# Tree attention on one Trainium2 core: products and transposes in couples of 64 columns, without the side-by-side copies

## The chip, the cores and the metric

The kernel runs on one core of one Trainium2 chip. The time is device time in microseconds (us), the median of several executions. The profile is one further execution, taken with the hardware profiler. Engines are named as the profile names them: PE is TensorE (PEld its weight loads), DVE is VectorE, ACT is ScalarE, POOL is GpSimd, SP is SyncE. "L561" is line 561 of the kernel.

## The reference

Attention over 8 x 12 = 96 heads of 512 positions by 64 numbers, fp32 in and out. Position i is a node of a binary tree and sees only itself and its ancestors:

```python
scale = 1.0 / np.sqrt(dim)
mask = np.zeros((seq, seq))
for i in range(seq):
    mask[i, i] = 1
    parent = i
    while parent > 0:
        parent = (parent - 1) // 2
        mask[i, parent] = 1
scores = np.einsum('bhqd,bhkd->bhqk', Q, K) * scale
scores = scores + (1 - mask) * (-1e9)
weights = np.exp(scores - np.max(scores, axis=-1, keepdims=True))
weights = weights / (np.sum(weights, axis=-1, keepdims=True) + 1e-10)
return np.einsum('bhqk,bhkd->bhqd', weights, V).astype(np.float32)
```

## The kernel before

The 96 heads are worked in 48 pairs; a pair's two heads lie on partitions 0 to 63 and 64 to 127 wherever 64 numbers of a head are the contraction. Four pairs (8 heads) are a group, the unit of loading: `load_k` and `load_q` bring 8 heads of K or Q, `load_v` 8 heads of V, from fp32 in memory to bf16 on the chip, all issued from GpSimd's queue. Results go out in fp32, 8 heads a store (`store`), and pair by pair for the last group (`store_pair`).

A pair passes through these steps:

- **Transposes** (`transpose_rows` for K, `transpose_coarse` for Q; L384 and L406, and L359 for the first group). TensorE turns K and Q of a group into columns, in four steps for a group, two of K and two of Q. VectorE copies the result out of PSUM (`evac`, tile `kq`). From group 3 on, a copy first lays the rows of two heads side by side (`lay_beside`, tiles `Kbeside` and `Qbeside`, L333), so that one transpose has 128 columns of weights and writes all 128 partitions: 8 transposes a step. In groups 0 to 2 there is no copy, and two transposes of 64 columns each write one half of the partitions: 16 a step. The copies of Q are GpSimd's, those of K VectorE's in groups 3 to 5 and GpSimd's from 6 on.
- **Scores** (`scores1`, `scores2`; L503, L508, L528, L534). Each query needs only a few blocks of keys. Codes added by extra products push the forbidden places far down. ScalarE takes the exponentials (L519, L550) into the tiles `e1` and `e2`.
- **Values** (`values`, L561). The exponentials are the weights of the array, 65 columns of V with a one behind them stream through; the 65th column of the result is the sum. For each head four products take `e1`, all 128 columns wide. Of the four that take `e2`, those with t = 2 and 3 are 128 wide; for t = 0 and 1 the two halves of the queries need different tiles of V (`SELF`), so each is two products of 64 columns. That is 20 products a pair, the 64-wide ones of both heads last.
- **Norm** (`norm`, L594 and L599): VectorE divides by the sum.

V is laid into five slots by copies of 32 or 64 partitions (`spread`, L309), shared out among GpSimd, VectorE and ScalarE by tables.

The order on each engine is written out by hand (`manual_schedule`): the main loop runs over pairs, with the steps S (scores of pair i), T (one step of transposes, some pairs ahead) and V (values and norm of pair i - 1); X is a filling product. GpSimd's order is the list of `pool_program`, one queue of loads, spreads, copies and stores in a fixed sequence; `ready` decides at which pair an entry may be written into the program. Loaded K and Q lie in `loads`, three buffers each, so a load of group g needs the buffer of group g - 3, which is free once that group's copy side by side is done. Stores are put some eight groups behind the loads (`BEHIND`), so in the last part of the kernel stores alone move.

Of the kernel before, what the change touches and what calls it, by code (L numbers as in the profile page):

```python
# [12 lines left out]
CODE_BITS = 16  # L13
NOUT = 10
BEHIND = 64
LANES = 8
COARSE = range(1, 12)
COARSE_K = range(1, 12)
BESIDE = {"K": range(3, 12), "Q": range(3, 12)}
K_BY_POOL = range(6, 12)  # L20


UNITS = (
# [101 lines left out]
def kernel(  # L125
# [36 lines left out]
    ctx.enter_context(tc.manual_schedule())  # L162

    consts = ctx.enter_context(tc.tile_pool(name="consts", bufs=1))
    loads = ctx.enter_context(tc.tile_pool(name="loads", bufs=3))
    beside = ctx.enter_context(tc.tile_pool(name="beside", bufs=2))
    vloads = ctx.enter_context(tc.tile_pool(name="vloads", bufs=3))
    work = ctx.enter_context(tc.tile_pool(name="work", bufs=2))
    etpool = ctx.enter_context(tc.tile_pool(name="etpool", bufs=3))
# [144 lines left out]
        for part in ((), (4, 5), (4, 5), (4, 5, 2))[min(o, 3)]:  # L314
            spread(nc.gpsimd.tensor_copy, o, part, h0, h1)

    besides = {}

    def lay_beside(copy, name, g):

        kept = (ksts if name == "K" else qsts)[g]
        to = besides[name, g] = beside.tile([P, GP, 4, 2, D], bf16, name=f"{name}beside")
        dst = to[:, :, :, :, :].bitcast(mybir.dt.uint32)
        src = kept[:, :, :, :].bitcast(mybir.dt.uint32)
        if g not in COARSE:
            src = src.rearrange("p (x a) t w -> p x t a w", a=2)
        elif name == "Q" or g in COARSE_K:
            src = src.rearrange("p a s w -> p s a w")
        else:
            src = src.rearrange("p (a x) t w -> p (x t) a w", a=2)  # L330
        if g in COARSE:
            dst = dst.rearrange("p x t a w -> p (x t) a w")
        copy(out=dst, in_=src)  # L333

    def lay_q(g):
        lay_beside(nc.gpsimd.tensor_copy, "Q", g)

    def lay_early(g):
        lay_beside(nc.gpsimd.tensor_copy, "K", g)

    halves_of, every = [slice(64 * a, 64 * a + 64) for a in range(2)], slice(0, P)

    def turned(name, g, t, both, single):

        if g in BESIDE[name]:
            return [(every, both(besides[name, g]).rearrange("p a d -> p (a d)"))]
        return [(halves_of[a], single(a)) for a in range(2)]

    def transpose_one(dst, rows, units, src, perm):

# [10 lines left out]
    def transpose_keys(i, kqp, half):  # L361
        g, x = divmod(i, GP)
        assert all(("kst", head(i, a)) in issued for a in range(2))
        for t in range(4):
            for rows, src in turned(
                "K", g, t, lambda b: b[:, x, t, :, :], lambda a: ksts[g][:, head(i, a) % KB, t, :]
            ):
                transpose_one(kqp[:, half, :, :], rows, _slot_layout(t)[1], src, perms[t])

    def transpose_rows(i, x):  # L370

        g = i // GP
        for half in range(2):
            j = 2 * x + half
            for t, (units, perm) in enumerate(runs):
                for rows, src in turned(
                    "K", g, t, lambda b: b[:, j, t, :, :], lambda a: ksts[g][:, a, 4 * j + t, :]
                ):
                    dst = kqps[i][rows, half, units[0], :]
                    dst = bass.AP(  # L380
                        dst.tensor, dst.offset,
                        [list(dst.ap[0])] + [[32 * (u - units[0]), 2] for u in units[2:0:-1]] + [[1, 32]],
                    )
                    nc.tensor.transpose(out=dst, in_=src, identity=perm)  # L384

    def transpose_coarse(i):

        g, x = divmod(i, GP)
        kqps[i] = kqps[i - 1] if x == 3 else psT.tile([P, 2, 32, 32], bf16, name="kqp")
        if x < 2 and g in COARSE_K:  # L390
            assert all(("kst", h) in issued for h in range(KB * g, KB * g + KB))
            return transpose_rows(i, x)
        if x < 2:
            for half in range(2):
                transpose_keys(GP * g + 2 * x + half, kqps[i], half)
            return
        assert all(("qst", h) in issued for h in range(KB * g, KB * g + KB))
        for half in range(2):
            for y, t in enumerate(ORDER):
                four = 2 * x - 4 + half  # L400
                for rows, src in turned(
                    "Q", g, t, lambda b: b[:, four, t, :, :], lambda a: qsts[g][:, a, 4 * four + t, :]
                ):
                    u = 16 * half + y
                    dst = kqps[i][rows, x - 2, u:u + 13:4, :]
                    nc.tensor.transpose(out=dst, in_=src, identity=eye[:, 0:128])  # L406

    def transpose(i, halves=(0, 1)):
        g = i // GP
        if g in COARSE:  # L410
            return transpose_coarse(i)
        if 0 in halves:
            kqps[i] = psT.tile([P, 2, 32, 32], bf16, name="kqp")
            transpose_keys(i, kqps[i], 0)
        assert all(("qst", h) in issued for h in (2 * i, 2 * i + 1))
        for y, t in enumerate(ORDER if 1 in halves else ()):
            for rows, src in turned(
                "Q", g, t, lambda b: b[:, i % GP, t, :, :], lambda a: qsts[g][:, 2 * i % KB + a, t, :]
            ):
                units = [2 * y, 2 * y + 1, 2 * y + 9, 2 * y + 10]  # L420
                transpose_one(kqps[i][:, 1, :, :], rows, units, src, qperm)

# [129 lines left out]
    def values(i):  # L552
# [4 lines left out]
            obs[i] = ob = psS.tile([P, 2, 512], fp32, name="s1")  # L557
        e1, e2, vt = ets[i], e2s[i % NE], vts[(2 * i // VB) % NV]

        def product(e, a, t, tile_v, lo=0, hi=128, **flags):  # L560
            nc.tensor.matmul(  # L561
                out=ob[lo:hi, a, 65 * t:65 * t + 65],
                lhsT=e[:, a, PLACE[t], lo:hi],
# [1 line left out]
                **flags,  # L565
            )

        def halves(a):
            for t in (0, 1):
                product(e2, a, t, 1 + SELF[t], 0, 64, start=False, stop=t == 1)  # L570
                product(e2, a, t, 1 + t, 64, 128, start=False, stop=t == 1)

        for a in range(2):
            for t in range(4):
                product(e1, a, t, 0, start=t == 0, stop=False)
            for t in (2, 3):
                product(e2, a, t, 1 + t, start=False, stop=False)
            if i == NP - 1:
                halves(a)
        if i < NP - 1:  # L580
            for a in range(2):
                halves(a)

    def norm(i):
        g = i // GP
# [34 lines left out]

    def pool_program():

        K_BEFORE = {
            6: (load_k, 8 * KB, KB), 10: (spread_top, 5, 0, KB), 11: (store, nc.gpsimd, 5),
        }

        Q_BEFORE = {
            3: (load_k, 5 * KB, KB), 4: (load_k, 6 * KB, KB), 5: (spread_top, 3, 0, KB), 6: (spread_top, 3, KB, VB),
            9: (spread_top, 4, KB, VB), 10: (spread_top, 5, KB, VB),
        }  # L630
        ops = [
            (load_k, 2, 2), (load_q, 2, 2), (load_v, 0, 8), (load_k, 4, 4),
            (load_q, 4, 2), (load_q, 6, 2), (load_k, 8, 8), (load_q, 8, 8), (eye_order,),
# [22 lines left out]
        ops.append((spread_top, NH // VB - 1, KB, VB))  # L656
        ops += [(store, nc.gpsimd, q) for q in range(stored, NH // KB - 1)]
        ops += [(store_pair, nc.gpsimd, i) for i in (NP - 4, NP - 3)]
        for g in BESIDE["Q"]:
            if g in Q_BEFORE:  # L660
                ops.insert(ops.index(Q_BEFORE[g]), (lay_q, g))
                continue
            at = ops.index((load_q, KB * g, KB)) + 1
            behind = 0
            while behind < LANES:
                behind += {load_k: 1, load_q: 1, load_v: 1, store: 2, store_pair: 1}.get(ops[at][0], 0)
                at += 1
            ops.insert(at, (lay_q, g))
        for g in K_BY_POOL:
            before = K_BEFORE.get(g, (lay_q, g))  # L670
            ops.insert(ops.index(before), (lay_early, g))
        return ops

    def ready(op, i):

        f, args = op[0], op[1:]
        if f in (load_k, load_q):
            g = args[0] // KB - 3
            name = "K" if f is load_k else "Q"
            return (name, g) in besides if g in BESIDE[name] else done >= GP * (g + 1)  # L680
        if f in (code_order, eye_order):
            return True
        if f in (lay_q, lay_early):
            return done >= GP * (args[0] - 1)
        if f is load_v:
            return 2 * i >= args[0] + args[1] - 3 * VB
        if f is spread_top:
# [58 lines left out]
                out=tile[:, 0, :], lhsT=idle[:, 0:128], rhs=idle[:, :], start=True, stop=True  # L746
            )

    def lay_k(i):

        for g in BESIDE["K"]:
            if g not in K_BY_POOL and i == K_TURN.get(g, GP * g - 7):
                lay_beside(nc.vector.tensor_copy, "K", g)

    spin("s1", 9)
    for kept, name, src in ((ksts, "kst", "K"), (qsts, "qst", "Q")):
        kept[0] = loads.tile([P, KB, 4, D], bf16, name=name)
        nc.vector.tensor_copy(out=kept[0][:, 0:2, :, :], in_=first[src][:, :, :, :])
    TWICE = (9,)
    K_TURN = {3: 7, 4: 10, 5: 14}  # L760
    FIRST = ['XKSQ', 'SXXXKXQDVAT', 'SVATT', 'SVTT', 'STV', 'STVD']
    done = 1
    pool(-1)
# [3 lines left out]
    for i in range(NP + 1):  # L767
        steps = FIRST[i] if i < len(FIRST) else "STVT" if i in TWICE else "SVT" if i == 8 else "STV"
        for n, step in enumerate(steps):
# [7 lines left out]
            if step == "T" and done < NP:  # L777
                transpose(done)
                evac(done)
                done += 1  # L780
                if "T" not in steps[n + 1:]:
                    lay_k(i)
            if step == "K":
                transpose(done, (0,))
            if step == "Q":
# [10 lines left out]
            spread_by(nc.vector.tensor_copy, BY_VECTOR, STEADY_VECTOR, i)  # L796
        if "A" not in steps:
            spread_by(nc.scalar.copy, BY_SCALAR, STEADY_SCALAR, i)
        if "T" not in steps:
            lay_k(i)  # L800
        pool(i)
        if i == NP - 1:
            store_pair(nc.sync, NP - 2)
# [33 lines left out]
```

## Time and profile before

| what | value |
|---|---|
| time, median of 3 runs | 133.08 us (133.0 to 133.45) |
| span of the profiled execution, first to last instruction | 131.9 us |
| what the median has beyond that span | 1.2 us |
| granted TensorE clock, mean | 0.993 |
| PE busy | 115.4 us in 2130 matmuls and transposes |
| DVE, ACT, POOL busy | 99.8, 94.1, 96.0 us |
| HBM read and written | 37.86 and 12.58 MB |

The profiled execution's own time is known as its span; what lies around the span is taken as the 1.2 us in the table. A row of the profile's groups reads: line, engine, operation, result <- operands, shapes, count, then busy time, mean duration of one in ns, then the engine's idle time just before and what ended it. Matmuls overlap each other, so a row's length is from the first's begin to the last's end. A row of the timeline or the chain reads: begin, length (us), engine, line, operation. Names such as `128*64 128x65` mean contraction rows * columns of the weights, then partitions x streamed columns.

### The profile page before, as it was taken

Reading aid. Unit: us, or ns where it says so; the run is one execution under the profiler, and the core shown is the slowest. Engines: PE = TensorE matmul, PEld = TensorE weight load, DVE = VectorE, ACT = ScalarE, POOL = GpSimd, SP = SyncE. Lnnn points to the kernel's source line nnn. Section 1 sums busy time; section 2 is a strip of 40 time slices with the busy share of each in tenths; the row PEclk is TensorE's granted clock in tenths of the full one; section 3 lists DMA queues with packets and bytes.
Section 4 is the critical chain, followed back from the end, with each engine's and each line's share of the span. In section 5 each row is a group of like instructions: output and inputs, shape, how many; then the busy total and the mean of one; then the engine's idle time right before and its main releaser. Section 6 shows DMA issues by size and latency. Waiting matters only on the chain.

```text
span 131.9 us, 4944 instructions
## 1 busy us (share of the span) xinstructions
PE 115.4 (88%) x2130; PEld 82.4 (62%) x2131; DVE 99.8 (76%) x191; ACT 94.1 (71%) x154; POOL 96.0 (73%) x147
## 2 busy tenths in 40 slices
PE   4989968899799879699999998999999999989930
PEld 1443645667566657477777776786877777856620
DVE  4339957774996897987988979879888799775460
ACT  4339345797766695778977889587888897979910
POOL 6999546049589899999999999699699998202300
PEclk9999999999999999999999999999999999999997
DMA  3999999999999999999999999999999989999991
GB/s 115 201 181 194 212 195 217 195 211 204 208 200 211 205 208 201 211 202 212 205 207 207 220 342 221 208 341 228 209 325 245 299 352 391 370 381 404 375 366 66
DMA packets 24533, 32.13 MB, mean 244 GB/s; under 512 B 944, under 2 KB 15920, under 8 KB 24512
## 3 DMA queue, kind: packets, MB, share of 16 engines
q0 software_dynamic: 23232, 30.67, 110.2%
q1 hardware_dynamic: 720, 0.70, 1.6%
q10 hardware_dynamic: 560, 0.46, 1.1%
q8 instruction: 16, 0.26, 0.7%
q14 instruction: 5, 0.04, 0.1%
HBM read 37.86 MB, written 12.58 MB: 382 GB/s over the span
## 4 chain that ended last, share of the span: by engine, by line
PE 63%; DVE 25%; ACT 6%; issue 3%; ACTq 0%
PE ob L561 18%; PE s L503 8%; PE kqp L406 8%; DVE of L599 7%; DVE kq L445 6%; PE s L508 6%; PE kqp L384 6%; PE s L528 6%; PE s L534 5%; DVE vt L309 4%; PE s L745 3%; ACT e L550 3%; ACT e L519 2%; PE kqp L359 2%; DVE kq L453 2%
## 5 line engine op out<-in xcount | busy, mean ns | idle before, releaser
L519 ACT ACTIVATE e<-s 128x1024 bf16<-128x1024 f32 x48 | 49.1, 1023 | 28.1 <-PE s L508 27.9
L309 POOL COPY vt<-vst 32x256 uint32<-32x256 uint32 (+2 forms) x70 | 36.1, 516 | 10.1 <-DMA vst<-in_V_dram 6.9
L550 ACT ACTIVATE e<-s 128x384 bf16<-128x384 f32 (+1 forms) x92 | 41.4, 505 | 0.0
L561 PE MATMUL ob<-vt,e 128*128 128x65 bf16 (+1 forms) x940 | 37.3, 197 | 3.2 <-DVE of L599 2.4
L561 PEld LDWEIGHTS <-e 128*128 128x128 bf16 (+1 forms) x960 | 31.2, 102 | 9.4 <-DVE of L599 4.8
L599 DVE TENSOR_TENSOR of<-ob,rec 128x512 f32<-128x512 f32 x44 | 30.4, 691 | 1.5
L309 DVE COPY vt<-vst 32x512 uint32<-32x512 uint32 (+4 forms) x43 | 23.2, 539 | 1.2
L594 DVE RECIPROCAL rec<-ob 128x8 f32<-128x8 f32 x47 | 9.5, 203 | 14.3 <-PE ob L561 13.5
L534 PEld LDWEIGHTS <-kq 64*128 64x128 bf16 x384 | 16.1, 110 | 6.4
L508 PE MATMUL s<-kq 64*128 64x512 bf16 x96 | 18.4, 378 | 1.3 <-DVE kq L445 1.3
L534 PE MATMUL s<-kq 64*128 64x160 bf16 (+1 forms) x384 | 17.8, 210 | 0.0
L503 PE MATMUL s<-qcoarse,codes 40*128 40x512 bf16 x88 | 17.2, 387 | 0.0
L528 PE MATMUL s<-qcoarse,codes 40*128 40x480 bf16 x88 | 16.3, 364 | 0.4 <-ACT e L550 0.2
L453 DVE COPY kq<-kqp 128x1024 bf16<-128x1024 bf16 x22 | 15.1, 687 | 2.0 <-PE kqp L384 1.3
L607 POOL DMA_DIRECT2D out_dram<-of x11 | 9.8, 893 | 8.5 <-DVE of L599 8.5
L445 DVE COPY kq<-kqp 128x2048 bf16<-128x2048 bf16 x11 | 13.5, 1224 | 2.4 <-PE kqp L406 1.8
L528 PEld LDWEIGHTS <-codes 40*128 40x128 bf16 x96 | 7.5, 95 | 9.1 <-issue 2.0
L384 PE MATMUL kqp<-mixed,Kbeside 128*128 128x128 bf16 x144 | 11.1, 220 | 1.8 <-DVE Kbeside L333 1.2
L333 POOL COPY Qbeside<-qst 128x1024 uint32<-128x1024 uint32 x9 | 9.7, 1081 | 2.6 <-DMA qst<-in_Q_dram 2.5
L406 PE MATMUL kqp<-ptile,Qbeside 128*128 128x128 bf16 x144 | 11.1, 220 | 0.4 <-DVE kq L453 0.4
L260 POOL DMA_DIRECT2D vst<-in_V_dram x12 | 10.9, 907 | 0.0
L384 PEld LDWEIGHTS <-Kbeside 128*128 128x128 bf16 x144 | 8.3, 98 | 3.2 <-DVE Kbeside L333 1.5
(45 smaller groups left out, 97.7 us busy)
## 6 DMA issues: line engine op xcount, KB each, us to landing
out_dram<-of POOLq DMA_DIRECT2D x11, 1024.0 KB, 9.9
vst<-in_V_dram POOLq DMA_DIRECT2D x12, 512.0 KB, 14.4
kst<-in_K_dram POOLq DMA_DIRECT2D x11, 512.0 KB, 12.2
qst<-in_Q_dram POOLq DMA_DIRECT2D x11, 512.0 KB, 13.2
out_dram<-ol POOLq DMA_DIRECT2D x2, 256.0 KB, 5.3
qst<-in_Q_dram POOLq DMA_DIRECT2D x3, 128.0 KB, 7.6
ol<-in_K_dram SPq DMA_DIRECT2D x1, 256.0 KB, 2.9
ol<-in_Q_dram ACTq DMA_DIRECT2D x1, 256.0 KB, 3.6
```

What stands on the lines that cost most here:

```text
L309: return copy(out=dst, in_=src)
L384: nc.tensor.transpose(out=dst, in_=src, identity=perm)
L406: nc.tensor.transpose(out=dst, in_=src, identity=eye[:, 0:128])
L445: return nc.vector.tensor_copy(out=dst, in_=src) if x == 3 else None
L503: nc.tensor.matmul(out=columns(g, sp[:, a, :], 0, 512), lhsT=k1code[64 * a:64 * a + CODE_ROWS, :], rhs=query_codes(i, a, 0, 0, 512), start ...
L508: nc.tensor.matmul(out=columns(g, sp[:, a, :], 0, 512), lhsT=keys(i, a, TOP), rhs=queries(i, a, 0, 512), start=False, stop=True,)
L519: nc.scalar.activation(out=dst, in_=src, func=AF.Exp, scale=scale)
L528: nc.tensor.matmul(out=columns(g, flat[:, a, :], 32, 512), lhsT=k2code[64 * a:64 * a + CODE_ROWS, :], rhs=query_codes(i, a, 1, 32, 512), s ...
L534: nc.tensor.matmul(out=columns(g, flat[:, a, :], lo, hi), lhsT=keys(i, a, TILE2[t]), rhs=queries(i, a, lo, hi), start=False, stop=t == 1,)
L550: nc.scalar.activation(out=dst, in_=src, func=AF.Exp, scale=scale)
L561: nc.tensor.matmul(out=ob[lo:hi, a, 65 * t:65 * t + 65], lhsT=e[:, a, PLACE[t], lo:hi], rhs=vt[:, head(i, a) % VB, tile_v, 0:D + 1], **flags,)
L599: nc.vector.tensor_tensor(out=dst, in0=o4[:, a:a + n, :, 0:D], in1=rec[:, a:a + n, :, :].to_broadcast([P, n, 4, D]), op=ALU.mult,)
```

## The change

Every transpose of K and Q and every value product becomes two of 64 columns, one for each half of the partitions. A pair takes 32 value products in place of 20, and a step of transposes 16 in all groups. The copies side by side, their buffers and their places in GpSimd's and VectorE's order go; the transposes of groups 3 to 11 read the loaded tiles themselves. `loads` has five buffers in place of three, and a load may be written once the transposes of five groups before have been. In the value step, all products of one head stand before those of the other, the `e1` products first.

```diff
-LANES = 8
-BESIDE = {"K": range(3, 12), "Q": range(3, 12)}
-K_BY_POOL = range(6, 12)
+LOADED = 5
...
-    loads = ctx.enter_context(tc.tile_pool(name="loads", bufs=3))
-    beside = ctx.enter_context(tc.tile_pool(name="beside", bufs=2))
+    loads = ctx.enter_context(tc.tile_pool(name="loads", bufs=LOADED))
...
-                for rows, src in turned(
-                    "K", g, t, lambda b: b[:, j, t, :, :], lambda a: ksts[g][:, a, 4 * j + t, :]
-                ):
+                for a, rows in enumerate(halves_of):
+                    src = ksts[g][:, a, 4 * j + t, :]
...
-                for rows, src in turned(
-                    "Q", g, t, lambda b: b[:, four, t, :, :], lambda a: qsts[g][:, a, 4 * four + t, :]
-                ):
+                for a, rows in enumerate(halves_of):
+                    src = qsts[g][:, a, 4 * four + t, :]
...
-        def halves(a):
-            for t in (0, 1):
-                product(e2, a, t, 1 + SELF[t], 0, 64, start=False, stop=t == 1)
-                product(e2, a, t, 1 + t, 64, 128, start=False, stop=t == 1)
-
         for a in range(2):
             for t in range(4):
-                product(e1, a, t, 0, start=t == 0, stop=False)
-            for t in (2, 3):
-                product(e2, a, t, 1 + t, start=False, stop=False)
-            if i == NP - 1:
-                halves(a)
-        if i < NP - 1:
-            for a in range(2):
-                halves(a)
+                for lo in (0, 64):
+                    product(e1, a, t, 0, lo, lo + 64, start=t == 0, stop=False)
+            for t in range(4):
+                for lo, of in ((0, SELF[t]), (64, t)):
+                    product(e2, a, t, 1 + of, lo, lo + 64, start=False, stop=t == 3)
...
-        for g in BESIDE["Q"]:
...
-            ops.insert(at, (lay_q, g))
-        for g in K_BY_POOL:
-            before = K_BEFORE.get(g, (lay_q, g))
-            ops.insert(ops.index(before), (lay_early, g))
         return ops
...
         if f in (load_k, load_q):
-            g = args[0] // KB - 3
-            name = "K" if f is load_k else "Q"
-            return (name, g) in besides if g in BESIDE[name] else done >= GP * (g + 1)
+            return done >= GP * (args[0] // KB - LOADED + 1)
```

More of the change, by code (lines that the diff above doesn't have):

```diff
@@ L315, in spread_top @@
             spread(nc.gpsimd.tensor_copy, o, part, h0, h1)
[L317 to L347, printed above, removed]
+    halves_of = [slice(64 * a, 64 * a + 64) for a in range(2)]
     def transpose_one(dst, rows, units, src, perm):
@@ L364, in transpose_keys @@
         for t in range(4):
-            for rows, src in turned(
-                "K", g, t, lambda b: b[:, x, t, :, :], lambda a: ksts[g][:, head(i, a) % KB, t, :]
-            ):
+            for a, rows in enumerate(halves_of):
+                src = ksts[g][:, head(i, a) % KB, t, :]
                 transpose_one(kqp[:, half, :, :], rows, _slot_layout(t)[1], src, perms[t])
@@ L400, in transpose_coarse @@
                 four = 2 * x - 4 + half
-                for rows, src in turned(
-                    "Q", g, t, lambda b: b[:, four, t, :, :], lambda a: qsts[g][:, a, 4 * four + t, :]
-                ):
+                for a, rows in enumerate(halves_of):
+                    src = qsts[g][:, a, 4 * four + t, :]
                     u = 16 * half + y
@@ L416, in transpose @@
         for y, t in enumerate(ORDER if 1 in halves else ()):
-            for rows, src in turned(
-                "Q", g, t, lambda b: b[:, i % GP, t, :, :], lambda a: qsts[g][:, 2 * i % KB + a, t, :]
-            ):
+            for a, rows in enumerate(halves_of):
+                src = qsts[g][:, 2 * i % KB + a, t, :]
                 units = [2 * y, 2 * y + 1, 2 * y + 9, 2 * y + 10]
@@ L558, in values, with product @@
         e1, e2, vt = ets[i], e2s[i % NE], vts[(2 * i // VB) % NV]
-        def product(e, a, t, tile_v, lo=0, hi=128, **flags):
+        def product(e, a, t, tile_v, lo, hi, **flags):
             nc.tensor.matmul(
@@ L621, in pool_program @@
     def pool_program():
[L623 to L630, printed above, removed]
         ops = [
@@ L658, in pool_program @@
         ops += [(store_pair, nc.gpsimd, i) for i in (NP - 4, NP - 3)]
-        for g in BESIDE["Q"]:
[L660 to L667, printed above, removed]
-            ops.insert(at, (lay_q, g))
-        for g in K_BY_POOL:
-            before = K_BEFORE.get(g, (lay_q, g))
-            ops.insert(ops.index(before), (lay_early, g))
         return ops
@@ L677, in ready @@
         if f in (load_k, load_q):
-            g = args[0] // KB - 3
-            name = "K" if f is load_k else "Q"
-            return (name, g) in besides if g in BESIDE[name] else done >= GP * (g + 1)
+            return done >= GP * (args[0] // KB - LOADED + 1)
         if f in (code_order, eye_order):
             return True
-        if f in (lay_q, lay_early):
-            return done >= GP * (args[0] - 1)
         if f is load_v:
@@ L747, in spin @@
             )
[L749 to L753, printed above, removed]
     spin("s1", 9)
@@ L759 @@
     TWICE = (9,)
-    K_TURN = {3: 7, 4: 10, 5: 14}
     FIRST = ['XKSQ', 'SXXXKXQDVAT', 'SVATT', 'SVTT', 'STV', 'STVD']
@@ L780 @@
                 done += 1
-                if "T" not in steps[n + 1:]:
-                    lay_k(i)
             if step == "K":
@@ L798 @@
             spread_by(nc.scalar.copy, BY_SCALAR, STEADY_SCALAR, i)
-        if "T" not in steps:
-            lay_k(i)
         pool(i)
```

## The prediction

> **What bounds the kernel now.** I read the page first: the engines' shares, the slices and the chain that ended last.
>
> ```profile
> span 131.9 us, 4944 instructions
> ...
> PE 115.4 (88%) x2130; PEld 82.4 (62%) x2131; DVE 99.8 (76%) x191; ACT 94.1 (71%) x154; POOL 96.0 (73%) x147
> ...
> DMA  3999999999999999999999999999999989999991
> GB/s 115 201 181 194 212 195 217 195 211 204 208 200 211 205 208 201 211 202 212 205 207 207 220 342 221 208 341 228 209 325 245 299 352 391 370 381 404 375 366 66
> ...
> q8 instruction: 16, 0.26, 0.7%
> ...
> PE 63%; DVE 25%; ACT 6%; issue 3%; ACTq 0%
> ```
>
> Two things are full at once. TensorE is busy 88% of the span and carries 63% of the chain. The DMA line reads 9 in nearly every slice from the second to the last but one. The rate in the first half, about 205 GB/s, is bf16 as written, so the fp32 read behind it is about 410 GB/s; in the eight slices before the last one fp32 results move, at 352 to 404 GB/s. So the DMA engines have no pause to give back, wherever it is that TensorE gets faster. The view by windows, for the last two stretches, shows where this ends:
>
> ```profile
> core 0: us, PE busy (x) PEld busy (x) DVE busy (x) ACT busy (x) POOL busy (x), PEclk, DMA share, GB/s
> 112.00:126.00 14.00, 13.08 (x263) 9.35 (x260) 8.78 (x19) 12.40 (x21) 3.20 (x4) 1.00 1.01 385
> 126.00:131.90 5.90, 0.39 (x10) 0.22 (x7) 1.46 (x5) 0.00 (x0) 0.00 (x0) 0.85 0.51 189
> ```
>
> From 112 to 126 us the stores run at 385 GB/s; in the last 5.90 us 189 GB/s, or 5.90 x 189 = 1.12 MB, are still moved. At 385 GB/s those would take 2.9 us, so with all results ready in time the bulk would be out at 126.0 + 2.9 = 128.9. The end of the present chain is this (timeline, and the view of DMA issues from 120 us on):
>
> ```profile
> 127.65 0.35 ACTq L616 DMA_DIRECT2D out_dram<-ol  x1
> ...
> out_dram<-of POOLq DMA_DIRECT2D x1, 1024.0 KB, 7.1
> ...
> out_dram<-ol ACTq DMA_DIRECT2D x1, 128.0 KB, 3.0
> ```
>
> The last store of a whole group lands 7.1 us after its issue, behind earlier ones. The very last store is issued at 127.65 and lands in 3.0 us, at 130.65; the span ends 1.25 us after that. It found no queue. So the end is set by the compute chain, but the DMA's own end is right under it: 128.9 for the bulk against 130.65 for the last landing.
>
> **The value products.** A pair now takes 12 products of 128 columns and 8 of 64; it will take 16 couples of 64. The timeline of one pair, cut by narrow windows so that the row shows only what had begun, an early pair that is followed by a half-width transpose, and one product by itself:
>
> ```profile
> 73.04 0.54 PE L561 MATMUL ob<-vt,e 128*128 128x65 bf16 x12
> 73.51 0.28 PE L561 MATMUL ob<-vt,e 128*64 128x65 bf16 x6
> 73.51 0.32 PE L561 MATMUL ob<-vt,e 128*64 128x65 bf16 x8
> ...
> 16.37 0.79 PE L561 MATMUL ob<-vt,e 128*128 128x65 bf16 x20
> 16.99 0.22 PE L384 MATMUL kqp<-mixed,kst 128*64 128x128 bf16 x2
> ...
> 75.17 0.19 PE L561 MATMUL ob<-vt,e 128*128 128x65 bf16 x1
> ```
>
> Twelve full products end at 73.58; with 0.19 us for one, the last begins at 73.39, so they follow at 0.35/11 = 0.032 us. The first half product begins at 73.51, 0.12 us after it and not 0.03: a change of width costs about 0.09 us. The fourth couple lengthens its row from 0.28 to 0.32; the whole row holds three steps, (0.32 - 0.19)/3 = 0.043 on average, the first of them the longest, since couples 2 to 4 can load weights behind running ones only once one runs. I take the later step as 0.032, that of a full product, which streams the same 65 columns, with 0.030 and 0.043 as ends. Sixteen couples then take 0.32 + 12 x 0.032 = 0.70 us against 0.79: a saving of 0.09 (0.11 at 0.030; at 0.043 the row is 0.84, a loss of 0.05).
>
> On weight loads the Trainium skill speaks against the change: the page "TensorEngine Tiling (Array Packing)", section Restrictions, says that column tiling rules out the fast weight load, and "TensorE: Matmul & The Clock Gate" gives a load as columns/1.2 ns, by which I estimate 53 ns for 64 columns and, if that were each couple's step, a pair of about 1.0 us. The rows above show steps far below that once couples run.
>
> **The transposes.** Groups 1 and 2 have the half form already, later groups the full one, so the profile shows both:
>
> ```profile
> 24.17 0.64 PE L384 MATMUL kqp<-mixed,kst 128*64 128x128 bf16 x16
> 24.74 0.20 PE L561 MATMUL ob<-vt,e 128*128 128x65 bf16 x1
> ...
> 74.71 0.62 PE L384 MATMUL kqp<-mixed,Kbeside 128*128 128x128 bf16 x8
> ```
>
> Sixteen halves take 0.64 us, eight fulls 0.62: +0.02 for a pair. With 0.22 for one transpose (the row at 16.99), the last half begins at 24.59 and the full product 0.15 later; the last full one begins at 75.11 and the product, at 75.17, 0.06 later. So the half form before full products costs 0.09 in a change of width. After the change products are half too and this falls away: in the 16.37 row products end at 17.16, the last begins at 16.97, and the half-width transpose begins 0.02 later. I charge nothing for it, so the step stays at 0.06 as now for groups 3 to 11. The scores stay as they are, and a change of width on entering and leaving them stays.
>
> The sum for a pair in the steady stretch is -0.09 + 0.02 = -0.07 us on TensorE (ends -0.09 and +0.07). What a pair takes now is in the chain:
>
> ```profile
> 86.70 0.61 PE ob L561 x20
> ...
> 88.82 0.61 PE ob L561 x20
> ...
> 125.36 1.04 PE s L561 x20
> ```
>
> A pair lasts 88.82 - 86.70 = 2.12 us, and all pieces between are TensorE's. From about 55 to 117 us the chain goes on like this, with some 28 such pairs: 28 x 0.07 = 2.0 us. The last pair changes width three times within 1.04 us; as 16 couples it takes 0.70, another 0.3 us on the very end.
>
> **Copies and buffers.** These rows (groups by form, and the waits) price what goes:
>
> ```profile
> L384 PE MATMUL kqp<-mixed,Kbeside 128*128 128x128 bf16 x144 | 11.1, 220 | 1.8 <-DVE Kbeside L333 1.2 <-DVE kq L445 0.3 <-DVE kq L453 0.3
> L406 PE MATMUL kqp<-ptile,Qbeside 128*128 128x128 bf16 x144 | 11.1, 220 | 0.4 <-DVE kq L453 0.4
> L333 POOL COPY Qbeside<-qst 128x1024 uint32<-128x1024 uint32 x9 | 9.7, 1081 | 2.6 <-DMA qst<-in_Q_dram 2.5
> L333 DVE COPY Kbeside<-kst 128x1024 uint32<-128x1024 uint32 x3 | 2.1, 687 | 0.0
> PEld L384 <- DVE Kbeside L333: 1.5, 2, 1.0
> ```
>
> VectorE loses three copies, 2.1 us, all before 55 us, and TensorE the 1.5 us it waits for two of them there. Part of that wait stands beside VectorE work that stays, so I count 1.0 (0 to 1.5). GpSimd loses nine Q copies, 9.7 us, and six K copies of like size. GpSimd is on no chain; what it gains is that loads and stores behind a copy are issued sooner. Their order in its one queue does not change: the copies are taken out of the list and all else stays. With a DMA queue that is never empty, a sooner issue lands nothing sooner. With three buffers a load waits for a copy of three groups before, with five for the transposes of five groups before, which were done long ago. So the buffers are worth 0 by themselves; they are what the longer-kept inputs need. If the queue ran dry somewhere, it would be around 105 us, and that would be a gain of a few tenths at most.
>
> TensorE's instructions rise: 576 more products (48 pairs x 12) and 288 more transposes, each with its weight load, 4261 to about 5990. The page has 16 fetches of instructions at 0.7% of 16 engines' span: 0.007 x 16 x 131.9 / 16 = 0.9 us of one DMA engine each. Seven more are 6.5 us of one engine, 0.4 us spread over sixteen; this delays the floor by 0.4 (0 if they fit into gaps, 0.9 if one falls on the engine that ends last).
>
> **The sum.** By the chain: -2.0 - 1.0 - 0.3 = -3.3 us. By the DMA: the bulk can be out at 128.9 + 0.4 = 129.3; if the last small stores land some 0.6 us behind it, at 129.9 where they now land at 130.65, and the 1.25 us after the landing stay, the span is 131.2. So of 3.3 us about 0.7 come through (0 to 1.7, the ends being no use of the floor's slack, and a last landing at 128.9 with no fetch charged). The median shown, 133.08, is 1.2 over the profiled span; I carry the difference over and round to 132.4.
>
> **Rivals.** (a) Nothing comes through: the fetches and the tail of small stores eat the 0.7. For it: DMA at 9 throughout, and the last 5.90 us already hold stores that queue for 7.1 us. Against: the last one lands in 3.0. It gives 132.7 to 133.4, so 133.0. (b) Slower: TensorE is not supplied with instructions or weights at the rate that sixteen couples want. A pair's products become 64 instructions, four for each couple; that is 0.032/4 = 0.008 us each, while the longest runs in the trace need one in 0.016 (twelve full products with their loads) or 0.42/32 = 0.013 (the sixteen half transposes). The four couples seen follow a pause of 0.12 us in which instructions can collect. It decides where a couple's step passes 0.039 us (0.79 - 0.02 - 0.19 = 0.58 over 15 steps). At 0.043 throughout, a pair loses 0.07, over 28 to 47 pairs 2 to 3.3 us: 135 to 136.4. At 0.013 per instruction a couple takes 0.052, the pair loses 0.20, and the time is 138.7 to 142.5. Against it: the fourth couple's step is 0.04 rounded, and the scores before each run leave time to collect. (c) The DMA is no floor: GpSimd's copies slowed it, and all 3.3 us come through: 129.8. The windows speak against it: from 112 to 126 us GpSimd works 3.20 of 14 us, and the DMA moves 385 GB/s, no more than the 410 before.
>
> The skill's rule that fits the gain is in "TensorEngine Tiling (Array Packing)", Key Properties: a change of tiling mode drains TensorE. The 0.12 against 0.03 above agrees.
>
> **How the numbers follow.** The forecast (the DMA lets through 0.7) has 0.52, (a) 0.21, (b) 0.21, (c) 0.06. A measurement of this kernel tells some 0.3% (0.4 us) from no change, so faster is below 132.7. The forecast's own range is 131.7 to 133.0, a tenth to a fifth of it above 132.7: faster 0.43 + 0.06 = 0.49; same 0.09 + 0.18 = 0.27; slower 0.03 + 0.21 = 0.24. The range runs from 131.6 to 136.4: it leaves out (c) and the harder half of (b), under 2 in 10.
>
> **What would show it.** Right: a product row of about 0.70 for 32 instructions and no pause of 0.12 within; half transposes of 0.64 followed by products after 0.06; pairs of 2.05 us; TensorE done some 3 us before its 126.4 of now, and the last store queueing for longer than 3.0 us. Wrong: couples that step by more than 0.039, idle time of TensorE put down to issue, a wait of transposes for K loads (then the loads have become late), or a DMA that shows gaps and an end that moves by 2 us or more.

## The result, and the profile after

The changed kernel takes 151.14 us (149.92 to 152.69, four runs) against 133.26 for the kernel before: a ratio of 1.129, 95% interval 1.119 to 1.139. It is slower by 18 us, where 0.7 us of gain were forecast. Each ratio here and below leaves out runs that are over 1.5% above the fastest of their kernel and goes by runs of the kernel before taken beside them, so it need not be the ratio of two medians shown. The profiled execution spans 148.5 us in place of 131.9. Its page:

```profile
span 148.5 us, 6661 instructions
...
PE 114.3 (77%) x2994; PEld 82.5 (56%) x2995; DVE 95.5 (64%) x188; ACT 94.3 (64%) x154; POOL 78.9 (53%) x132
...
DMA  4999999999999999999999999999708998043284
...
q8 instruction: 23, 0.38, 1.0%
...
PE 58%; issue 13%; DMA 10%; DVE 8%; ACT 5%; POOL 3%; ACTq 0%; POOLq 0%
```

TensorE is not busier than before (114.3 against 115.4 us), though it has 2994 matmuls and transposes in place of 2130. It stands still more. "issue", time in which the engine waited for nothing that the profile shows, was 3% of the chain and is 13%, and DMA, which was not in the chain, is 10%. The fetches of instructions rose from 16 to 23, as forecast. The waits say where TensorE stood:

```profile
PE ob L524 <- issue: 11.3, 8, 2.3
...
PE s L497 <- issue: 3.7, 2, 2.2
...
PE kqp L349 <- issue: 2.6, 2, 1.5
...
PE kqp L349 <- DMA kst<-in_K_dram: 1.7, 1, 1.7
...
PE kqp L370 <- issue: 1.5, 1, 1.5
PE s L471 <- issue: 1.0, 1, 1.0
```

Fifteen gaps of 0.5 to 2.3 us, 21.8 us in all, in value products, scores and transposes alike. They bear no relation to what the program does at that place. The timeline shows one, in the middle of a row of products, and a row without one:

```profile
56.84 0.67 PE L524 MATMUL ob<-vt,e 128*64 128x65 bf16 x32
...
58.95 0.60 PE L524 MATMUL ob<-vt,e 128*64 128x65 bf16 x27
61.10 0.26 PE L524 MATMUL ob<-vt,e 128*64 128x65 bf16 x5 [1.54 <-issue]
...
62.23 0.64 PE L370 MATMUL kqp<-ptile,qst 128*64 128x128 bf16 x16
62.71 0.68 PE L524 MATMUL ob<-vt,e 128*64 128x65 bf16 x32
```

An undisturbed row of 32 products takes 0.67 to 0.68 us. The row of 58.95 stops after 27 of them until 61.10. What these gaps have in common is their distance, counted in instructions. Cutting the windows at points inside the gaps (54.9, 60.8 and, at the gap before a single product at 66.92, 66.6) gives the number between them:

```profile
54.90:60.80 5.90, 4.39 (x128) 3.35 (x128) 4.16 (x8) 4.21 (x7) 5.51 (x11) 1.00 1.26 205
60.80:66.60 5.80, 4.39 (x128) 3.36 (x127) 3.57 (x6) 4.20 (x7) 4.38 (x9) 1.00 1.18 207
```

A row of such a window reads: stretch, length, then busy time and number of instructions of PE, PEld, DVE, ACT and POOL, the granted clock, the DMA's share and GB/s. 128 matmuls and 128 weight loads are 256 instructions, and a fetch of instructions is 16 KB (0.38 MB in 23), 64 bytes for each of 256. The transfer of one begins at 58.8, ends at 59.7, and TensorE goes on at 61.10; the next begins at 64.7 (DMA windows of 0.1 us there hold one packet of the instruction queue each), and TensorE goes on at 66.92. So the transfer of a block begins 3.6 us after TensorE steps into the block before it (55.17 and 61.10), takes 0.95, and 1.3 us more pass until its instructions run: 5.9 us from one block to the next, in which TensorE works for 4.39. The granted clock is 1.00 in both windows, so it is not the clock that makes them long. Where it does fall, to 0.72 from 91.5 to 97.5 us, the block takes 6.0 us as well, but TensorE is busy for 5.61 of them and no gap stands at its end.

The DMA's 10% of the chain is the same thing under another name:

```profile
76.86 14.84 DMA kst<-in_K_dram
91.69 0.20 issue
91.89 0.24 PE kqp L349
```

TensorE does stand before this transpose, but its K (group 8, issued at 58.8, 14.0 us to landing) had been there since 72.8; the load issued at 76.86 is K of group 10, which this transpose does not read. A fetch had begun at 89.5, and by count the transpose is the first instruction of a new block. In the kernel with loads cut in two, further below, the same transpose stands for the same 1.74 us, and there the profile names VectorE. So both names are the profile's guess at a wait for a block.

### The profile page after: what moved, and what is told of

The parts are those of the page before. It is cut to its first block, busy times and chain, and to the rows that moved or that the text cites. A ratio compares the mean times of both kernels' runs of the same rounds, so it can differ in the third digit from the quotient of the medians.

```text
span 148.5 us, 6661 instructions
## 1 busy us (share of the span) xinstructions
PE 114.3 (77%) x2994; PEld 82.5 (56%) x2995; DVE 95.5 (64%) x188; ACT 94.3 (64%) x154; POOL 78.9 (53%) x132
## 4 chain that ended last, share of the span: by engine, by line
PE 58%; issue 13%; DMA 10%; DVE 8%; ACT 5%; POOL 3%; ACTq 0%; POOLq 0%
PE ob L524 14%; DMA kst<-in_K_dram 10%; PE s L466 8%; PE kqp L349 7%; PE kqp L370 6%; PE s L491 6%; PE s L471 6%; PE s L497 5%; PE s L675 3%; DVE kq L408 2%; POOL vt L306 2%; ACT e L482 2%; ACT e L513 2%; PE kqp L326 2%; PE ob L675 1%
## 5 line engine op out<-in xcount | busy, mean ns | idle before, releaser
L482 ACT ACTIVATE e<-s 128x1024 bf16<-128x1024 f32 x48 | 49.2, 1024 | 43.1 <-PE s L471 42.9
L306 POOL COPY vt<-vst 32x256 uint32<-32x256 uint32 (+2 forms) x70 | 34.4, 491 | 33.9 <-PE ob L524 16.7
L524 PE MATMUL ob<-vt,e 128*64 128x65 bf16 x1504 | 34.4, 196 | 12.4 <-issue 11.3
L524 PEld LDWEIGHTS <-e 128*64 128x64 bf16 x1536 | 30.8, 112 | 14.7 <-issue 12.1
L497 PEld LDWEIGHTS <-kq 64*128 64x128 bf16 x384 | 16.9, 111 | 11.1 <-issue 4.6
L497 PE MATMUL s<-kq 64*128 64x160 bf16 (+1 forms) x384 | 18.6, 212 | 3.7 <-issue 3.7
L306 DVE COPY vt<-vst 32x512 uint32<-32x512 uint32 (+4 forms) x43 | 20.5, 477 | 1.2
L349 PE MATMUL kqp<-mixed,kst 128*64 128x128 bf16 x352 | 14.7, 225 | 5.6 <-issue 2.6
L466 PE MATMUL s<-qcoarse,codes 40*128 40x512 bf16 x88 | 17.4, 391 | 0.2 <-ACT e L482 0.2
L370 PE MATMUL kqp<-ptile,qst 128*64 128x128 bf16 x352 | 14.2, 222 | 1.8 <-issue 1.5
L349 PEld LDWEIGHTS <-kst 128*64 128x64 bf16 x352 | 11.0, 111 | 7.5 <-issue 4.4
L370 PEld LDWEIGHTS <-qst 128*64 128x64 bf16 x352 | 10.7, 109 | 3.7 <-issue 2.2
```

Source lines behind the costliest of these rows:

```text
L306: return copy(out=dst, in_=src)
L466: nc.tensor.matmul(out=columns(g, sp[:, a, :], 0, 512), lhsT=k1code[64 * a:64 * a + CODE_ROWS, :], rhs=query_codes(i, a, 0, 0, 512), start ...
L482: nc.scalar.activation(out=dst, in_=src, func=AF.Exp, scale=scale)
L497: nc.tensor.matmul(out=columns(g, flat[:, a, :], lo, hi), lhsT=keys(i, a, TILE2[t]), rhs=queries(i, a, lo, hi), start=False, stop=t == 1,)
L524: nc.tensor.matmul(out=ob[lo:hi, a, 65 * t:65 * t + 65], lhsT=e[:, a, PLACE[t], lo:hi], rhs=vt[:, head(i, a) % VB, tile_v, 0:D + 1], **flags,)
```

## The experiments

The fetch theory: where the DMA is loaded, TensorE gets 256 instructions in about 6.0 us and no more, so a group of four pairs takes at least 11.6 us after (496 instructions) and 7.9 before (336), where the group measured below took 9.0. A pair has 14 score products, 20 value products and 8 transposes before, 32 and 16 of the last two after, each with a weight load: 84 and 124 instructions. The expectations below count four too few for every pair (80 and 120, and so on), which moves their least times by 0.4 us a group and no verdict. The rivals: couples cannot be supplied for long whatever the DMA does (couple theory); or the missing copies and five buffers changed the order of loads so that something starves (buffer theory).

**One half of the change at a time.** First the value products alone as couples; then transposes, copies and buffers alone. The first (v_only) is the kernel before with this edit in `values`; the second (t_only) is the kernel after with this edit taken back:

```diff
-                product(e1, a, t, 0, start=t == 0, stop=False)
-            for t in (2, 3):
-                product(e2, a, t, 1 + t, start=False, stop=False)
-            if i == NP - 1:
-                halves(a)
-        if i < NP - 1:
-            for a in range(2):
-                halves(a)
+                for lo in (0, 64):
+                    product(e1, a, t, 0, lo, lo + 64, start=t == 0, stop=False)
+            for t in range(4):
+                for lo, of in ((0, SELF[t]), (64, t)):
+                    product(e2, a, t, 1 + of, lo, lo + 64, start=False, stop=t == 3)
```

> Only the value products become couples; transposes, side-by-side copies and three buffers stay as before. A group of four pairs then has 4 x 104 = 416 TensorE instructions (before 4 x 80 = 320, after 4 x 120 = 480). Fetch theory (TensorE streams its instructions in blocks of 256, and with the DMA busy one block takes about 6.0 us from request to use): a group cannot be shorter than 416 x 6.0 / 256 = 9.75 us, against 9.0 us in before; over 8 groups +6 us, so 137 to 142 us, with idle time of TensorE at every 256th instruction of about 0.5 to 1 us each. Buffer theory (the new order of loads and the missing copies starve the transposes): no change from before or a little faster, 132 to 133.5 us. Couple theory (a couple cannot be supplied at 0.03 us for long): the row of 32 products is itself longer than 0.79 us.

> Only the transposes become couples, the copies go and there are five buffers; value products stay 12 full and 8 half. A group has 4 x 96 = 384 instructions. Fetch theory: at least 384 x 6.0 / 256 = 9.0 us a group, just what a group takes now, plus 0.09 us per pair for the change of width between transposes and full products: 0 to +5 us, 133 to 138 us, with small stalls at every 256th instruction. Buffer theory: all of the loss is here, 148 to 152 us.

Couples of values alone: 140.22 us, ratio 1.057 (1.049 to 1.065). Transposes, copies and buffers alone: 133.51, ratio 1.003 (0.999 to 1.007), no difference that can be told. Removing the copies and adding buffers costs nothing, so the buffer theory falls; but five small gaps, 2.3 us in all, are put down to issue in its trace, where the kernel before has none in its main loop. With couples for the values alone, a value row without a gap takes 0.70 us (0.67 to 0.68 in the kernel after, 0.79 for 20 products), so couples are not slow in themselves; the gaps are there, shorter, and a block apart:

```profile
61.59 0.70 PE L561 MATMUL ob<-vt,e 128*64 128x65 bf16 x32
...
83.89 0.60 PE L561 MATMUL ob<-vt,e 128*64 128x65 bf16 x26
85.55 0.28 PE L561 MATMUL ob<-vt,e 128*64 128x65 bf16 x6 [1.05 <-issue]
...
79.20:85.20 6.00, 4.85 (x128) 3.65 (x128) 4.04 (x7) 4.00 (x8) 4.85 (x6) 1.00 1.19 211
85.20:91.30 6.10, 5.50 (x128) 4.08 (x128) 4.80 (x10) 4.14 (x7) 5.10 (x9) 1.00 1.16 295
```

**The kernel after with fewer products.** All of after, with couples on the second exponentials left out, eight (`E2_TILES` = 0) or four (2) of the sixteen, down to 92 and to 108 instructions a pair:

```diff
-            for t in range(4):
+            for t in range(E2_TILES):
                 for lo, of in ((0, SELF[t]), (64, t)):
...
```

> The kernel after, with the eight couples of each pair that take the second exponentials left out (the result is not the reference's); couples, half-width transposes, five buffers, no copies, all loads and stores stay. A pair has 88 TensorE instructions, a group 352. Fetch theory: 352 x 6.0 / 256 = 8.25 us a group would do, less than a group takes anyway, so no idle time at the 256th instructions and 131.5 to 133.5 us, that is, the loss of 18 us is gone. If the loss lies in half width, missing copies or buffers, most of it stays: 145 us or more.

> The same with only four of the sixteen couples of a pair left out: 104 instructions a pair, as many as the kernel with couples for the values alone. Fetch theory: 416 x 6.0 / 256 = 9.75 us a group and the time of that kernel, 138 to 142 us, although its transposes, copies and buffers are others. Any theory by kind of instruction: closer to after, 146 to 150.

With 92 instructions: 133.39 us, ratio 1.001 (0.996 to 1.005). With 108: 139.43, ratio 1.045 (1.038 to 1.052), near the couples of values alone with their 108. Two kernels with different transposes, copies and buffers agree within 1% at the same count. By kind of instruction nothing fits: eight couples a pair, and all half-width transposes, cost nothing here.

The kernels side by side. The group is measured from the first K transposes of group 3 to those of group 11, divided by 8; its instructions are twice the weight loads that the trace has between these marks, divided by 8 (the stretch holds about 31 pairs, not 32):

| kernel | instructions a pair | instructions in the measured group | group, us | us per 256 | ratio of times |
|---|---|---|---|---|---|
| before | 84 | 323 | 9.0 | 7.1 | 1 |
| after, 8 couples left out | 92 | 358 | 8.95 | 6.4 | 1.001 |
| transposes alone | 100 | 388 | 9.06 | 6.0 | 1.003 |
| values alone | 108 | 413 | 9.53 | 5.9 | 1.057 |
| after, 4 couples left out | 108 | 418 | 9.83 | 6.0 | 1.045 |
| after | 124 | 478 | 11.17 | 6.0 | 1.129 |

From 388 instructions a group up, 256 of them take 5.9 to 6.0 us whatever the kernel is; below that something else decides. The kernel with the new transposes alone has the time of before, yet it already stands at the limit, which fits its small gaps.

**The kernel after with a free DMA.** Loads beyond the first 48 heads are left out in both kernels (shown for K and Q; that of V is alike):

```diff
+        if h0 >= LAST_LOADED:
+            kept[h0 // KB] = kept[h0 // KB - 3]
+            return
...
```

> The kernel after, with no loads of K, Q and V beyond the first 48 heads: later groups work on tiles that are still there, so the result is not the reference's. TensorE's instructions are those of after. Fetch theory: from about 55 us on the DMA is idle apart from stores, a block's fetch begins about 1.2 us after its request in place of 3.7, and the stalls vanish there; a group takes 8.1 to 8.6 us in place of 11.2, and the whole 122 to 132 us. Couple theory (the sequencer itself is too slow for so many instructions): the groups stay near 11 us, 148 to 152.

> The kernel before without loads of K, Q and V beyond the first 48 heads (the result is not the reference's): what is left when the DMA is free. If the DMA was a floor right under the chain, as the prediction had it, TensorE's chain stays as it is and only the stores' tail shortens: 130 to 132.5 us. Beside the kernel after with the same loads left out it also tells what couples are worth where blocks of instructions come in time: groups of 8.6 us there against 8.7 to 9.0 here.

The kernel after takes 138.33 us, ratio 1.040 (1.034 to 1.046), more than the 122 to 132 forecast, and before 132.64, ratio 0.987 (0.982 to 0.993). The windows from 55 to 100 us, first of after, then of after without these loads:

```profile
55.00:100.00 45.00, 35.32 (x963) 26.50 (x964) 28.60 (x56) 28.81 (x48) 28.08 (x49) 0.96 1.21 241
```

```profile
55.00:100.00 45.00, 44.53 (x1307) 34.18 (x1304) 38.58 (x74) 38.82 (x66) 24.88 (x44) 1.00 0.25 97
```

The same program, with the DMA share at 0.25 in place of 1.21, runs 2611 TensorE instructions in these 45 us in place of 1927, and the gaps at the blocks are gone. So neither couples nor the sequencer are slow; what is slow is the way of a block through a loaded DMA. 45 us for 1927 are 23.4 ns each, 6.0 us for 256. The gaps that stay, 7.6 us in place of 21.8, lie where the DMA is full: four before 50 us, where the loads stayed, and one at 109 us, when stores alone fill it:

```profile
108.91 0.28 PE L531 MATMUL ob<-vt,e 128*64 128x65 bf16 x6
112.13 0.38 PE L531 MATMUL ob<-vt,e 128*64 128x65 bf16 x7 [2.93 <-issue]
```

**Behind what a fetch waits.** Loads of K and Q cut into two transfers each:

```diff
+        for part in range(2):
+            nc.gpsimd.dma_start(
+                out=to[:, part, :, :].rearrange("p s d -> p (s d)"),
+                in_=src[32 * h0 + P * part:32 * h0 + P * (part + 1), :],
+            )
...
```

> The kernel after, with each load of K and Q from group 1 on cut into two transfers of half the size; same bytes, same instructions on TensorE. It asks behind what a block's fetch waits 3.7 us. If it waits for whole transfers that were begun (512 KB take about 2.5 us), the wait falls to about 2.5 us, a block to 4.8 us, a group to 480 x 4.8 / 256 = 9.0 us, and the time to 135 to 141 us. If it waits behind a fixed amount of data inside the DMA engines, the wait stays at 3.7 and the time at 148 to 153 us.

151.83 us, ratio 1.143 (1.137 to 1.150): no gain. From 55 to 100 us TensorE ran 952 + 950 instructions, as few as after. So the wait does not go by the size of a K or Q transfer; the loads of V (512 KB) and the stores (1024 KB) stayed whole. What it goes by is open.

**More instructions with the same work.** This was to be the opposite test: the work of before with the instructions of after. Neither way gave an answer.

```diff
+            for _ in range(IDLE_OPS):
+                nc.tensor.nop(nofuse=True)
```

> The kernel before, with two instructions that do nothing behind each value product, 40 for a pair: 4 x 120 = 480 instructions a group, as many as after, and the same matmuls, copies and loads as before. Fetch theory: as slow as after, 146 to 154 us, with stalls of 1 to 2.5 us at every 256th instruction. Couple theory and buffer theory: 133 to 134 us, or, if the empty instructions take time of their own, a loss that lies evenly inside the value rows and not in single long gaps.

132.84 us, ratio 0.998 (0.995 to 1.001). But the page counts 4944 instructions, as before: the empty ones never came to the chip. The run says nothing of the fetch; it is one more run of before. Then padding by alignment:

```diff
             if step == "S" and i < NP:
+                nc.tensor.addr_align(SLOTS)
```

> The kernel before, with an alignment of TensorE's instruction stream ahead of each pair's scores, so that a pair fills 128 slots in place of 80; the padding is empty instructions, and matmuls, copies, loads and their order are those of before. Fetch theory: a group of four pairs is 512 slots and cannot be shorter than 512 x 6.0 / 256 = 12.0 us while the DMA is busy (9.0 now): about 24 us more, 150 to 160 us, with a fetch about every 6 us and one long gap for each. Any theory that lays the loss on couples, on missing copies or on five buffers: 133 to 134 us.

> The same padding to 128 slots a pair, and no loads of K, Q and V beyond the first 48 heads (later groups use tiles that are still there, so the result is not the reference's). It tells what the empty instructions cost by themselves. Fetch theory: a stretch of slow groups until about 50 us, then groups of 8.5 to 9.2 us without long gaps while the DMA is idle. If the padding itself takes the time, the groups stay at 11 to 12 us throughout.

312.07 us, and 314.47 without the loads: ratios of 2.35 and 2.37. The padding takes time by itself. The page counts 2433 more instructions than before (7377 against 4944), and TensorE stands for 128.8 us ahead of the scores with the loads and 128.9 without them: 53 ns for each empty instruction, whether the DMA is loaded or not. The rest lies in TensorE's own work, 172.4 us busy in place of 115.4, at a granted clock of 0.62. So these two tell nothing of the fetch either.

**The last pair alone.**

```diff
+COUPLES = 47
...
+        for a in range(2 if i >= COUPLES else 0):
+            for t in range(4):
+                for lo in (0, 64):
+                    product(e1, a, t, 0, lo, lo + 64, start=t == 0, stop=False)
...
+        if i >= COUPLES:
+            return
         for a in range(2):
```

> The kernel before, with the value products of the very last pair alone as couples: 12 more products, 24 more instructions, nothing else. The last pair's row falls from 1.04 to 0.7 us and lies on the end of the chain; no block has to be fetched for it in time. Fetch theory: 0.2 to 0.4 us faster, 132.7 to 132.9 where before has 133.1 (a ratio of 0.997 to 0.999, at the limit of what can be told). If couples are slow by themselves: 133.1 to 133.5.

133.48 us, ratio 1.002 (0.999 to 1.006): no gain. The timeline and the chain's end show why:

```profile
125.27 0.87 ACT L551 ACTIVATE e<-s 128x384 bf16<-128x384 f32 x2
...
125.50 1.01 PE L562 MATMUL s<-vt,e 128*64 128x65 bf16 x32
...
125.95 0.69 DVE ol L610
126.64 0.10 DVE rec L605
126.74 0.02 issue
126.76 0.42 DVE ol L610
127.19 0.10 DVE rec L605
127.29 0.02 issue
127.31 0.42 DVE ol L610
```

The row of 32 products takes 1.01 us and not 0.70: ScalarE's last exponentials run until 126.14 (125.27 + 0.87), and the products that take them end at 126.51. The row of the last pair is as long in the kernel after, 1.06 us. And a shorter row would meet a busy VectorE: it norms pair 46 until 126.64 and then the two heads of pair 47 one behind the other, with no wait for TensorE between them.

## Why the prediction was wrong

**The step that failed** is the one on TensorE's instructions: "Seven more are 6.5 us of one engine, 0.4 us spread over sixteen; this delays the floor by 0.4". It counted the blocks rightly (23 for 16) and priced them as load on the DMA engines. What they cost is latency: TensorE waits for the block. With 0.9 us for a transfer the price looked harmless; the whole way is 6.0 us, and that sets a least time of 23.4 ns an instruction. Before, a pair of 84 instructions in 2.12 us used 25.2, so it sat just above this limit without a gap to show it. A pair of 124 needs 2.90. In the groups of the table this is 8 x (11.17 - 9.0) = 17.4 us, and the span grew by 16.6 (148.5 - 131.9). The prediction had "idle time of TensorE put down to issue" among its signs of being wrong, and it is the sign that came.

The Trainium skill has the mechanism: "Runtime: NRT & Kernel Launch", section Instruction fetch mechanics, says that each engine streams its program in blocks of 256 instructions by a DMA queue of its own, and fetches the next while it works on the current one. The blocks of 256 agree with the counts above. It also says that crossing into a block is mostly hidden; here that holds at 25.2 ns an instruction and ends at 23.4 while the DMA is loaded.

**Rival (b)** came nearest and had the wrong limit. It asked whether couples are supplied fast enough, and looked for the limit inside a row, at 0.013 us an instruction. Rows were never the place: a row of 32 products runs at its full rate, 64 instructions in 0.68 us. The limit holds over blocks, at nearly twice that time per instruction, and the time of 151 lies outside all that the rival priced (135 to 142.5).

**Right in the terms, without effect on the sum.** The product row fell from 0.79 to 0.67 or 0.68 (0.70 forecast); half transposes take 0.64, and the products begin 0.06 after the last of them (62.23 + 0.64 - 0.22 = 62.65, then 62.71). But this pair, without a gap, still takes 2.12 us (transposes at 62.23 and at 64.35), not 2.05: its second scores begin at 63.83, just behind ScalarE's exponentials, which run until 63.78. With the later loads left out, groups 5 to 9, from K transpose to K transpose, take 8.6 us each in the kernel after and 8.9 in the kernel before. That is 0.07 us a pair, the size that was forecast for couples and transposes; so a gain of that size is there where the blocks come in time, and it is small beside the 18 us.

**The last pair's 0.3 us** were no gain. The prediction took the length of the row, 1.04 us, for changes of width; the row waits for ScalarE's last exponentials, and couples leave it at 1.01 to 1.06 us.

**The DMA as a floor under the chain** is borne out. With 92 instructions a pair TensorE ran ahead, until it stood before K of groups 10 and 11:

```profile
94.22 0.58 PE L350 MATMUL kqp<-mixed,kst 128*64 128x128 bf16 x14 [2.09 <-DMA kst<-in_K_dram]
...
105.50 0.47 PE L350 MATMUL kqp<-mixed,kst 128*64 128x128 bf16 x10 [3.40 <-DMA kst<-in_K_dram]
```

These loads landed at 94.2 and 105.5, so here the wait is real. With half the value products gone, that kernel still takes the time of before. **Copies and buffers** brought nothing that can be told, neither the buffers' 0 nor the copies' 1.0 us on the chain: 1.003 for the kernel that changes only these and the transposes. As that kernel stands at the limit of the blocks, the copies' 1.0 us is not priced by itself.

None of the versions that do the whole work beats the kernel before.

## What to carry to other kernels

Count an engine's instructions beside its work. In a kernel that keeps the DMA full, a stretch cannot run faster than its instruction blocks come (here 256 in 6.0 us), and a kernel just above that limit shows nothing of it; cutting products in two is then paid for even where each couple runs as fast as one whole. Idle time marked "issue", at places that have nothing in common but their distance of 256 instructions, is the sign, and a wait put down to a DMA that landed long ago may be the same gap.

## What was not expected of the hardware

- A block's way is long because the DMA is loaded. In the kernel after, its transfer begins mostly 3.6 to 3.8 us after TensorE steps into the block before, where loads fill the DMA. Where they do not, it begins sooner: 1.2 us after the step at 109.76 in that kernel, and 0.3 to 0.6 us after it from 55 to 70 us with the later loads left out. The transfer itself is 0.9 to 1.1 us in all these cases.
- The wait did not change when loads of K and Q were cut in half (1902 instructions in 45 us against 1927).
- An empty padding instruction holds TensorE for about 53 ns (128.8 us for 2433), over three times the 0.016 us an instruction of a row of full products.
